# Layer 0's causal mask from a matmul with a constant, and low weight halves on GpSimd

## The chip, the cores and the metric

The kernel runs on one core of a Trainium2 chip. The metric is the device time of one execution in microseconds. A core has five engines with queues of their own that run in order: TensorE (PE, with its weight loads shown apart as PEld), VectorE (DVE), ScalarE (ACT), GpSimd (POOL) and SyncE (SP, which here only issues DMAs).

## The reference

Two layers of a decoder trunk over 512 tokens of width 1024. The change touches the mixer of layer 0 alone: stick-breaking attention of 8 heads of width 64 beside a short convolution of 512 channels, both fed by one projection.

```python
def stick_breaking_attention(q, k, v):
    ...
        z = jnp.einsum('bqhd,bkhd->bhqk', qb, k).astype(jnp.float32) * scale
        mask = kpos[None, :] < qpos[:, None]
        log_beta = jax.nn.log_sigmoid(z)
        log_1m_beta = jnp.where(mask, log_beta - z, 0.0)
        after = lax.cumsum(log_1m_beta, axis=3, reverse=True) - log_1m_beta
        w = jnp.where(mask, jnp.exp(log_beta + after), 0.0)
        return jnp.einsum('bhqk,bkhd->bqhd', w.astype(v.dtype), v)
```

In words: each weight is the sigmoid of its logit times the product of (1 - sigmoid) of all later keys that the query may see. A key at or after the query's own place counts as 1 in the product and as 0 in the weight. After layer 0's mixer come a SwiGLU, layer 1's sparse attention and a second SwiGLU, which the change leaves alone.

## The kernel before

Products are made in three matmuls of fp32r halves: weights and inputs are split into a rounded high half and a low half (`mm3`, L105 to L107; token-major L232 to L234). A weight tile of 128 x 1024 numbers is loaded to `raw`, ScalarE rounds it to `wh` (L162), and an engine takes `raw - wh` to `wl` (L163): VectorE, unless the caller names another in `lo`. `raw`, `wh` and `wl` have three buffers each, and a tile feeds 24 matmuls of 512 columns.

Layer 0's mixer (`layer0_mix`) runs in this order: the queries, then key and value projections (`k_proj`, `proj_tm`), four key tiles in all, then four convolution chunks of three tiles each (`conv_chunk`). The attention heads are a generator (`stick`) that is stepped between groups of three projection matmuls, so that heads and projection share every engine's queue. For a head and a block of 128 queries, `first` makes the logits `z` on TensorE (L507, L508), two sigmoids on ScalarE (`om` = 1 - sigmoid, L525, and `be` = sigmoid, L526), two masks on GpSimd on the diagonal block (L528: 1 into `om`, 0 into `be`) and a column of ones (L531), then a scan of products over `om` (L532) and the product with `be` (L535) on VectorE. `second` turns `be` on TensorE (`pt`, L552), splits it (`wth` on ScalarE, L184; `wtl` on VectorE, L185) and multiplies by the values (`po`, L562, L563); ScalarE and VectorE then take `po` out (`ptmp`, `o`). `k_proj` scales its product to `kt` (L648) and lays each of two heads' keys into both halves of the partitions: one half by ScalarE (L651), the other by GpSimd (L652); VectorE makes the low half (L653).

A tile framework sets the order of most of this stage by its own estimates; the engines then run their queues in that order. `plan` cuts the first key tile and the first value tile ahead, on VectorE.

Of the kernel before, what the change touches and what calls it, by code (L numbers as in the profile page):

```python
# [8 lines left out]
F32 = mybir.dt.float32  # L9
F32R = mybir.dt.float32r  # L10
ALU = mybir.AluOpType
# [65 lines left out]
class Net:  # L77
# [238 lines left out]
    def setup(self):  # L316
        nc, I = self.nc, self.I
        cst = self.cst
        self.ones = cst.tile([P, P], F32, name="ones")
        nc.vector.memset(self.ones, 1.0)  # L320
        self.zero = cst.tile([P, 1], F32, name="zero")
        nc.vector.memset(self.zero, 0.0)
        self.ssq = cst.tile([P, S], F32, name="ssq")
        one = self.ssq[:, 2 * P:3 * P]
        nc.gpsimd.affine_select(out=one, in_=self.ones, pattern=[[-1, P]],
                                compare_op=ALU.is_equal, fill=0.0, base=0, channel_multiplier=1)
        self.eye = cst.tile([P, P], F32R, name="eye")
        nc.vector.tensor_copy(self.eye, one)
        self.ident = self.eye.bitcast(F32)
        self.xT = cst.tile([P, KC, S], F32, name="xT")  # L330
        self.rbc = cst.tile([P, S], F32, name="rbc")
        self.rcol = cst.tile([P, TB], F32, name="rcol")
        self.rq = cst.tile([P, 2 * TB], F32, name="rq")
        self.arena = cst.tile([P, int(ARENA_KB * 256)], F32R, name="arena")

        rows, self.rows2 = self.ssq[0:16, 0:P], self.ssq[0:32, P:2 * P]
        self.cols = cst.tile([P, 48], F32, name="cols")
        nc.scalar.dma_start(rows, I["norm_mix"].rearrange("l (c p) -> (l c) p", p=P))
        nc.scalar.activation(self.rcol[:, 0:1], self.zero, AF.Copy, scale=self.ones[:, 0:1])

        warm = self.bank("z", "pstat")
        for i in range(WARM):
            nc.tensor.matmul(warm[:, 0:P], self.ones, self.ones, start=True, stop=True)
        ps = self.bank("z", "pstat")
        nc.tensor.transpose(ps[:, 0:16], rows, self.ident[0:16, 0:16])
        nc.vector.tensor_copy(self.cols[:, 0:16], ps[:, 0:16])
# [163 lines left out]
    def stick(self, heads, keys, sp, state):  # L510


        nc = self.nc
        outs = {}

        def first(h, qb, ws):
            i, e = h // 2, h % 2
            qs, (kd, kl) = heads[i], keys[i]
            nk = (qb + 1) * P
            t = slice(qb * P, nk)  # L520
            z = self.bank("z", "z")[:, 0:nk]
            self.qk(z, qs[:, e, t], kd[:, e, 0:nk], kl[:, e, 0:nk])
            om = sp.tile([P, nk + 1], F32, name="om", tag=f"om{qb}", bufs=1)
            be = sp.tile([P, nk], F32, name="be", tag=f"be{qb}", bufs=2)
            nc.scalar.activation(om[:, 0:nk], z, AF.Sigmoid, scale=self.rq[:, qb:qb + 1])  # L525
            nc.scalar.activation(be, z, AF.Sigmoid, scale=self.rq[:, TB + qb:TB + qb + 1])  # L526
            for tile_, fill in ((om, 1.0), (be, 0.0)):
                nc.gpsimd.affine_select(out=tile_[:, t], in_=tile_[:, t], pattern=[[-1, P]],  # L528
                                        compare_op=ALU.is_gt, fill=fill, base=0,
                                        channel_multiplier=1)  # L530
            nc.gpsimd.memset(om[:, nk:nk + 1], 1.0)  # L531
            nc.vector.tensor_tensor_scan(om[:, 0:nk][:, ::-1], om[:, 0:nk][:, ::-1],  # L532
                                         self.zero.to_broadcast([P, nk]), initial=1.0,
                                         op0=ALU.mult, op1=ALU.add)
            nc.vector.tensor_tensor(be, be, om[:, 1:nk + 1], op=ALU.mult)  # L535
            ws[qb] = be

        def second(h, ws):
            i, e = h // 2, h % 2
            rows = slice(64 * e, 64 * e + 64)  # L540
            po = self.bank("c" if h % 2 and state["acc"] else "o", "po")

            def turn(kbs, j):
                self.turns += 1
                pt = self.bank("tb"[self.turns % 2] if state["acc"] else "t", "pt")
                wh = sp.tile([P, S], F32R, name="wth", tag="wth", bufs=4)
                wl = sp.tile([P, S], F32R, name="wtl", tag="wtl", bufs=4)
                n, place = 0, {}
                for kb in kbs:
                    place[kb] = n  # L550
                    for qb in range(kb, TB):
                        nc.tensor.transpose(pt[:, n:n + P], ws[qb][:, kb * P:(kb + 1) * P],  # L552
                                            self.ident)
                        n += P
                self.split((wh[:, 0:n], wh.bitcast(F32)[:, 0:n], wl[:, 0:n]), pt[:, 0:n])
                return wh, wl, place

            def prod(kbs, wh, wl, place):
                for kb in kbs:
                    a = slice(place[kb], place[kb] + (TB - kb) * P)  # L560
                    v = self.vs[:, kb, h]
                    nc.tensor.matmul(po[:, kb * P:], v, wh[:, a], start=kb == 0, stop=False)  # L562
                    nc.tensor.matmul(po[:, kb * P:], v, wl[:, a], start=False, stop=kb == 2)  # L563

            groups = ((0,), (1, 3), (2,))
            t0 = turn(groups[0], 0)
            yield True
            t1 = turn(groups[1], 1)
            yield True
            while not state["v"]:  # L570
                yield False
            prod(groups[0], *t0)
            t2 = turn(groups[2], 0)
            yield True
            prod(groups[1], *t1)
            yield True
            prod(groups[2], *t2)

            if e == 0:
                outs[i] = sp.tile([P, S], F32, name="o", tag="o")  # L580
            tmp = sp.tile([P, S], F32, name="ptmp", tag="ptmp")
            nc.scalar.copy(tmp[rows], po[64:128])
            nc.vector.tensor_tensor(outs[i][rows], po[0:64], tmp[rows], op=ALU.add)
            if e == 1:
                (ah, ahf), al = self.R(32 + 4 * i, S), self.R(34 + 4 * i, S)[0]
                self.split((ah, ahf, al), outs[i])
            yield True

        prev = iter(())
        for h in range(9):  # L590
            ws = {}
            if h < 8:
                while not state["k"] > h // 2:
                    yield False
                for qb in range(TB):
                    first(h, qb, ws)
                    yield True
                    r = next(prev, None)
                    while r is False:
                        yield False  # L600
                        r = next(prev, None)
                    if r:
                        yield True
            yield from prev
            prev = second(h, ws) if h < 8 else None

    def layer0_mix(self):
# [28 lines left out]
        with self.tc.tile_pool(name="l0", bufs=1) as sp:  # L636
# [5 lines left out]
            def k_proj(i):  # L642
                b = 64 + 8 * (i % 3)
                (kd, kdf), kl = self.R(b, 2, S), self.R(b + 4, 2, S)[0]

                def ev_k(m, ps):
                    kt = sp.tile([P, S], F32, name="kt", tag="ct0")
                    nc.vector.tensor_tensor(kt, ps, self.rbc, op=ALU.mult)  # L648
                    for e in range(2):
                        own, oth = slice(64 * e, 64 * e + 64), slice(64 - 64 * e, 128 - 64 * e)  # L650
                        nc.scalar.copy(kd[own, e], kt[own])  # L651
                        nc.gpsimd.tensor_copy(kd[oth, e], kt[own])  # L652
                        nc.vector.tensor_tensor(kl[own, e], kt[own], kdf[own, e], op=ALU.subtract)  # L653
                self.proj_fm(W, 512 + i * P, P, xs, ev_k, gcols=P, per=8)
                return kd, kl

            conv = []
# [3 lines left out]
            def conv_chunk(j):  # L661
# [24 lines left out]
                    self.split((ah, ahf, al), y)  # L686

                for col, ev in ((2048, ev_c), (2560, ev_u), (1536, ev_b)):
                    self.proj_fm(W, col + j * P, P, xs, ev, gcols=P, per=8)
                conv.append((ah, al))  # L690

            def more_keys():
# [3 lines left out]
            for i in range(4):  # L696
# [4 lines left out]
                    self.few_banks(None)  # L701
                self.after(LAG0, more_keys)
                if i == 0:
                    self.proj_tm(W, 1024, xs, ev_v)
                    self.after(LAG0, lambda: state.update(v=True))
                    self.few_banks("ad")
                    state["acc"] = True
# [532 lines left out]
```

## Time and profile before

| what | us |
|---|---|
| median of three runs (1211.82 to 1212.19) | 1211.86 |
| the profiled execution | 1214.13 |
| its span on the core | 1212.4 |
| TensorE busy in the span | 1189.0 |
| VectorE, ScalarE, GpSimd busy | 652.9, 480.1, 143.8 |

A row of a group of instructions gives line, engine, operation, tiles written and read, shape, count, then busy time and mean nanoseconds of one, then the idle time of that engine just before them and what ended it. A row of the timeline gives start, duration, engine, line, operation and tiles. Durations of matmuls overlap: what one costs in a stream is the distance to the next start.

### The profile page before, as it was taken

The page shows a single profiled execution, that of the slowest core. Times are in us where ns is not written, and L with a number is a line of the kernel's source. Part 1 is how long each engine was busy: PE and PEld are TensorE (multiplying, and loading weights), DVE is VectorE, ACT ScalarE, POOL GpSimd, SP SyncE. Part 2 cuts the span into 40 slices and gives each one's busy share as a digit, 9 for nine tenths or more (in the row PEclk, how much of TensorE's full clock was granted, in tenths as well). Part 3 has the DMA queues.
Part 4 walks back from the last instruction along what each step waited for, and adds up shares of the span by engine and source line. Part 5 has one row for each costly group of instructions (what it writes and reads, how often), then busy time and mean ns, then how long its engine had stood idle before and what let it go on. Part 6 is the DMA issues. An engine that isn't in the chain of part 4 may idle for free.

```text
span 1212.4 us, 14654 instructions
## 1 busy us (share of the span) xinstructions
PE 1189.0 (98%) x5547; PEld 978.5 (81%) x5547; DVE 652.9 (54%) x1067; ACT 480.1 (40%) x797; POOL 143.8 (12%) x217
## 2 busy tenths in 40 slices
PE   9999999999999999999999989999999999999998
PEld 7777878888888888888788868888888888888886
DVE  5679965655545443333379977745444343342222
ACT  5556634543434332222253577534332322322120
POOL 1234300200000000011001554312000000000000
PEclk9999999999999999999999999999999999999999
DMA  5322125878887632232346432223333333332430
GB/s 191 92 70 70 53 84 190 277 248 281 284 273 262 226 92 96 96 96 78 124 150 232 157 104 70 71 78 126 91 89 90 103 87 102 89 104 88 129 97 35
DMA packets 118583, 159.86 MB, mean 132 GB/s; under 512 B 6292, under 2 KB 91840, under 8 KB 118512
## 3 DMA queue, kind: packets, MB, share of 16 engines
q1 hardware_dynamic: 117712, 157.73, 40.1%
q10 hardware_dynamic: 800, 1.18, 0.3%
q8 instruction: 44, 0.72, 0.2%
q14 instruction: 27, 0.22, 0.1%
HBM read 131.00 MB, written 27.89 MB: 131 GB/s over the span
## 4 chain that ended last, share of the span: by engine, by line
PE 89%; DVE 6%; issue 2%; POOL 2%; ACT 0%; DMA 0%; POOLq 0%; DVEq 0%; ACTq 0%
PE acc L105 22%; PE acc L107 21%; PE acc L106 21%; PE acc L234 6%; PE acc L233 6%; PE acc L232 6%; PE pt L1118 1%; PE z L507 1%; PE z L508 1%; DVE om L532 1%; DVE wl L163 1%; PE po L106 1%; PE po L107 1%; DVE be L535 1%; PE po L105 1%
## 5 line engine op out<-in xcount | busy, mean ns | idle before, releaser
L105 PE MATMUL acc<-arena,wh 128*128 128x512 f32 (+2 forms) x1176 | 466.7, 397 | 1.9 <-DVE xT L728 1.0
L107 PE MATMUL acc<-arena,wl 128*128 128x512 f32 (+2 forms) x1176 | 458.2, 390 | 0.1
L106 PE MATMUL acc<-arena,wh 128*128 128x512 f32 (+2 forms) x1176 | 458.0, 389 | 0.0
L163 DVE TENSOR_TENSOR wl<-raw,wh 128x1024 fp32r<-128x1024 f32 (+1 forms) x167 | 202.9, 1215 | 285.3 <-ACT wh L162 285.0
L162 ACT CAST wh<-raw 128x1024 fp32r<-128x1024 f32 (+1 forms) x167 | 173.0, 1036 | 360.5 <-PE acc L106 155.7
L107 PEld LDWEIGHTS acc<-arena,wl 128*128 128x128 f32 (+1 forms) x1176 | 220.4, 187 | 49.9 <-DVE wl L163 0.4
L105 PEld LDWEIGHTS acc<-arena,wh 128*128 128x128 f32 (+1 forms) x1176 | 220.8, 188 | 46.9 <-DVE xT L728 2.1
L106 PEld LDWEIGHTS acc<-arena,wh 128*128 128x128 f32 (+1 forms) x1176 | 220.8, 188 | 43.6 <-issue 0.7
L232 PE MATMUL acc<-wh,arena 128*128 128x512 f32 x272 | 108.8, 400 | 0.0
L234 PE MATMUL acc<-wh,arena 128*128 128x512 f32 x272 | 108.4, 399 | 0.0
L233 PE MATMUL acc<-wl,arena 128*128 128x512 f32 x272 | 108.2, 398 | 0.0
L286 POOL TENSOR_TENSOR ssq<-ssq,sqx 128x512 f32<-128x512 f32 x12 | 18.2, 1520 | 371.7 <-ACT sqx L285 371.7
L234 PEld LDWEIGHTS acc<-wh,arena 128*128 128x128 f32 x272 | 51.5, 189 | 12.2
L815 DVE TENSOR_TENSOR pwl<-praw,pwh 128x1024 fp32r<-128x1024 f32 (+1 forms) x25 | 30.2, 1208 | 57.0 <-ACT pwh L814 57.0
L233 PEld LDWEIGHTS acc<-wl,arena 128*128 128x128 f32 x272 | 51.5, 189 | 11.6
L232 PEld LDWEIGHTS acc<-wh,arena 128*128 128x128 f32 x272 | 51.5, 189 | 11.5
L763 DVE TENSOR_TENSOR ft<-acc,rbc 128x512 f32<-128x512 f32 x44 | 30.0, 690 | 45.7 <-PE acc L107 45.6
L814 ACT CAST pwh<-praw 128x1024 fp32r<-128x1024 f32 (+1 forms) x25 | 25.9, 1036 | 68.5 <-DMA praw<-in_od_w_in_dram 38.2
L765 ACT ACTIVATE fs<-ft 128x512 f32<-128x512 f32 x44 | 27.6, 629 | 51.3 <-DVE ft L763 51.3
L507 PE MATMUL z<-arena 128*128 128x384 f32 (+3 forms) x120 | 40.7, 342 | 6.7 <-DVE mx L1085 4.1
L1085 DVE CUSTOM_DVE_ANT_0 L<-z,bias 128x128 f32<-128x128 f32 (+3 forms) x64 | 30.7, 485 | 22.2 <-PE z L1084 19.6
L770 DVE TENSOR_TENSOR fp<-acc,fs 128x512 f32<-128x512 f32 x44 | 30.4, 690 | 22.7 <-PE acc L107 22.7
(212 smaller groups left out, 1281.0 us busy)
## 6 DMA issues: line engine op xcount, KB each, us to landing
raw<-in_ffn_w_gate_dram SPq DMA_DIRECT2D x44, 512.0 KB, 3.7
raw<-in_ffn_w_up_dram SPq DMA_DIRECT2D x44, 512.0 KB, 3.8
raw<-in_ffn_w_down_dram SPq DMA_DIRECT2D x42, 512.0 KB, 3.7
l1h<-pwh SPq DMA_DIRECT2D x24, 512.0 KB, 2.7
l1l<-pwl SPq DMA_DIRECT2D x24, 512.0 KB, 3.1
wh<-l1h SPq DMA_DIRECT2D x24, 512.0 KB, 4.0
wl<-l1l SPq DMA_DIRECT2D x24, 512.0 KB, 4.5
raw<-in_ev_w_in_dram SPq DMA_DIRECT2D x23, 512.0 KB, 3.9
```

Source lines behind the costliest of these rows:

```text
L105: mm(ps, wh, xh, start=first, stop=False)
L106: mm(ps, wh, xl, start=False, stop=False)
L107: mm(ps, wl, xh, start=False, stop=last)
L162: nc.scalar.copy(wh, raw)
L163: (lo or nc.vector).tensor_tensor(wl, raw, wh.bitcast(F32), op=ALU.subtract)
L232: mm(ps[tb], h[:, t], wh[:, k], start=c == 0, stop=False)
L233: mm(ps[tb], h[:, t], wl[:, k], start=False, stop=False)
L234: mm(ps[tb], l[:, t], wh[:, k], start=False, stop=c == kc - 1)
L507: self.nc.tensor.matmul(z, qs, kd, start=True, stop=False)
L770: nc.vector.tensor_tensor(p, ps, sil[m], op=ALU.mult)
L815: nc.vector.tensor_tensor(l, raw, h.bitcast(F32), op=ALU.subtract)
L1085: nc.vector.tensor_tensor_reduce(out=u["ls"][:, r], in0=z, in1=bias[h][:, 0:nk][:, ::-1], scale=1.0, scalar=FILL, op0=ALU.add, op1=ALU.max ...
```

## The change

The diagonal mask becomes a third matmul into the logits: the identity (`eye`) times a constant `ahead` that holds -1e30 at and above the diagonal. The sigmoids then give 1 and 0 there by themselves. The GpSimd masks and the 32 small memsets go; four `om` tiles get their ones once. The low halves of key tiles 1 to 3, value tiles 1 to 3 and all twelve convolution tiles go from VectorE to GpSimd: 18 tiles (the two that are cut ahead stay). For the first key tile the copy to the other half of the partitions goes from GpSimd to VectorE.

```diff
+        far = self.ssq[:, 3 * P:4 * P]
+        nc.gpsimd.memset(far, 0.0)
+        nc.gpsimd.affine_select(out=far, in_=far, pattern=[[-1, P]], compare_op=ALU.is_gt,
+                                fill=NEG, base=0, channel_multiplier=1)
+        self.ahead = cst.tile([P, P], F32R, name="ahead")
+        nc.gpsimd.tensor_copy(self.ahead, far)
...
+        oms = [sp.tile([P, (qb + 1) * P + 1], F32, name=f"om{qb}", bufs=1) for qb in range(TB)]
+        for qb in range(TB):
+            nc.gpsimd.memset(oms[qb][:, (qb + 1) * P:], 1.0)
...
-            self.qk(z, qs[:, e, t], kd[:, e, 0:nk], kl[:, e, 0:nk])
-            om = sp.tile([P, nk + 1], F32, name="om", tag=f"om{qb}", bufs=1)
+            self.qk(z, qs[:, e, t], kd[:, e, 0:nk], kl[:, e, 0:nk], False)
+            nc.tensor.matmul(z[:, t], self.eye, self.ahead, start=False, stop=True)
+            om = oms[qb]
...
-            for tile_, fill in ((om, 1.0), (be, 0.0)):
-                nc.gpsimd.affine_select(out=tile_[:, t], in_=tile_[:, t], pattern=[[-1, P]],
-                                        compare_op=ALU.is_gt, fill=fill, base=0,
-                                        channel_multiplier=1)
-            nc.gpsimd.memset(om[:, nk:nk + 1], 1.0)
...
-                        nc.gpsimd.tensor_copy(kd[oth, e], kt[own])
+                        (nc.gpsimd if i else nc.vector).tensor_copy(kd[oth, e], kt[own])
...
-                self.proj_fm(W, 512 + i * P, P, xs, ev_k, gcols=P, per=8)
+                self.proj_fm(W, 512 + i * P, P, xs, ev_k, gcols=P, per=8, lo=nc.gpsimd)
...
-                    self.proj_fm(W, col + j * P, P, xs, ev, gcols=P, per=8)
+                    self.proj_fm(W, col + j * P, P, xs, ev, gcols=P, per=8, lo=nc.gpsimd)
...
-                    self.proj_tm(W, 1024, xs, ev_v)
+                    self.proj_tm(W, 1024, xs, ev_v, lo=nc.gpsimd)
```

Line numbers of the changed kernel are 6 or 7 higher. TensorE's queue at the first head's logits, before (`acc` is the value projection, 128x128 and 128x256 the first two query blocks):

```order
L507 MATMUL z<-arena 128x128
L507 MATMUL z<-arena 128x256
L234 MATMUL acc<-wh,arena 128x512
L232 MATMUL acc<-wh,arena 128x512
L233 MATMUL acc<-wl,arena 128x512
L234 MATMUL acc<-wh,arena 128x512
L508 MATMUL z<-arena 128x128
L508 MATMUL z<-arena 128x256
```

The same place after:

```order
L513 MATMUL z<-arena 128x128
L513 MATMUL z<-arena 128x256
L234 MATMUL acc<-wh,arena 128x512
L232 MATMUL acc<-wh,arena 128x512
L514 MATMUL z<-arena 128x128
L534 MATMUL z<-ahead,eye 128x128
L514 MATMUL z<-arena 128x256
L534 MATMUL z<-ahead,eye 128x128
```

Two projection matmuls that stood ahead of the second logit product now stand behind it, and each block has its mask matmul. By the fourth turned block (`pt`) 20 projection matmuls have gone since the first logit before, 13 after. From the second head's last logits on, heads and projection stand in the same order in both, to within one matmul, but for the mask matmuls.

VectorE's queue in the first convolution chunk, before:

```order
L675 TENSOR_TENSOR cg<-acc,ct 128x512
L163 TENSOR_TENSOR wl<-raw,wh 128x1024
L678 SCALAR_TENSOR_TENSOR cy<-cg,cols,cy 128x512
L532 SCALAR_TENSOR_TENSOR om<-om,zero 128x384
L680 SCALAR_TENSOR_TENSOR cy<-cg,cols,cy 128x512
L535 TENSOR_TENSOR be<-be,om 128x384
L682 TENSOR_TENSOR cy<-cy,rbc 128x512
L185 TENSOR_TENSOR wtl<-pt,wth 128x256
```

And after:

```order
L682 TENSOR_TENSOR cg<-acc,ct 128x512
L539 SCALAR_TENSOR_TENSOR om_408<-om_408,zero 128x384
L685 SCALAR_TENSOR_TENSOR cy<-cg,cols,cy 128x512
L542 TENSOR_TENSOR be<-be,om_408 128x384
L687 SCALAR_TENSOR_TENSOR cy<-cg,cols,cy 128x512
L185 TENSOR_TENSOR wtl<-pt,wth 128x256
L689 TENSOR_TENSOR cy<-cy,rbc 128x512
```

The weight's low half is gone from the queue, and the scan and the low half of the turned block stand one place earlier among the convolution's own steps. GpSimd's queue from the first `om` memset on, before:

```order
L531 MEMSET om 128x1 x4
L672 MEMSET cg 128x2
L652 CAST arena<-kt 64x512 x2
L528 AFFINE_SELECT om<-om 128x128
L528 AFFINE_SELECT be<-be 128x128
L528 AFFINE_SELECT om<-om 128x128
L531 MEMSET om 128x1
```

And after, where `wl` are the weights' low halves:

```order
L163 TENSOR_TENSOR wl<-raw,wh 128x1024 x2
L524 MEMSET om_406 128x1
L524 MEMSET om_407 128x1
L524 MEMSET om_408 128x1
L524 MEMSET om_409 128x1
L679 MEMSET cg 128x2
L163 TENSOR_TENSOR wl<-raw,wh 128x1024 x4
L659 CAST arena<-kt 64x512 x2
L163 TENSOR_TENSOR wl<-raw,wh 128x1024
```

Two low halves of value tiles stand ahead of the memsets; the third value tile's stands right behind them.

## The prediction

> **What bounds the kernel now.** I read the page's busy totals first, then a table of stretches around the changed stage, then TensorE's waits there.
>
> ```profile
> span 1212.4 us, 14654 instructions
> PE 1189.0 (98%) x5547; PEld 978.5 (81%) x5547; DVE 652.9 (54%) x1067; ACT 480.1 (40%) x797; POOL 143.8 (12%) x217
> 43.50:62.00 18.50, 15.58 (x66) 11.29 (x66) 10.81 (x18) 8.59 (x15) 7.60 (x20) 0.91 0.23 65
> 62.00:108.00 46.00, 44.07 (x213) 35.70 (x214) 39.11 (x56) 28.81 (x51) 18.81 (x41) 1.00 0.24 69
> 108.00:161.00 53.00, 50.84 (x264) 41.77 (x263) 50.69 (x79) 33.72 (x64) 17.05 (x47) 1.00 0.21 60
> 161.00:275.00 114.00, 114.00 (x499) 93.14 (x498) 67.75 (x78) 49.42 (x61) 9.59 (x7) 1.00 0.65 214
> ...
> PE po L563 <- DVE wtl L185: 2.9, 3, 1.4
> PE pt L552 <- DVE be L535: 2.1, 4, 0.6
> ```
>
> In a row of stretches come start and end, length, busy time of PE, PEld, DVE, ACT, POOL, then TensorE's granted clock. TensorE is the bound everywhere, so a change gains only by closing its idle time and loses by each matmul that it adds. The heads of layer 0 run from 43.5 to 161 us. There TensorE is idle 18.5 - 15.58 = 2.9 us in the first stretch (at a clock of 0.91) and 46 - 44.07 + 53 - 50.84 = 4.1 us in the two others; behind 161 us it has no gap. So about 7 us plus the slow clock is all that can be had. The two wait rows (from 43.5 to 165 us; total, times, longest) say who ends most of the gaps: VectorE's two results for the turned blocks, 5.0 us. One GpSimd copy, below, ends the rest. VectorE is the close second: 39.11 + 50.69 = 89.8 us busy of 99.
>
> **The mask matmuls.** 32 are added, one for each head and block. Their price is the distance between starts in a stream. The same form stands in layer 1, a constant times the identity:
>
> ```profile
> 700.80 0.30 PE L507 MATMUL z<-arena 128*128 128x128 f32 x1 [0.35 <-DVE mx L1085]
> 700.93 0.28 PE L508 MATMUL z<-arena 128*128 128x128 f32 x1
> 701.04 0.28 PE L507 MATMUL z<-arena 128*128 128x128 f32 x1
> 702.77 0.28 PE L508 MATMUL z<-arena 128*128 128x256 f32 x1
> 702.89 0.28 PE L1084 MATMUL z<-mask,eye 128*128 128x256 f32 x1
> ```
>
> Starts 0.11 to 0.13 us apart for 128 columns, 0.12 for 256: the narrow ones are no cheaper than the wide. I take 0.11, so 32 x 0.11 = 3.5 us; the low end is half of the 256-column distance, 32 x 0.06 = 1.9, the high end 32 x 0.13 = 4.2. All 32 lie in TensorE's stream, so they are paid unless they fall into a gap.
>
> **What leaves GpSimd and VectorE.**
>
> ```profile
> L163 DVE TENSOR_TENSOR wl<-raw,wh 128x1024 fp32r<-128x1024 f32 x15 | 19.5, 1301 | 2.6 <-ACT wh L162 2.6
> L528 POOL TENSOR_SCALAR_AFFINE_SELECT be<-be 128x128 f32<-128x128 f32 x32 | 19.2, 598 | 5.0 <-ACT be L526 4.5
> L528 POOL TENSOR_SCALAR_AFFINE_SELECT om<-om 128x128 f32<-128x128 f32 x32 | 13.5, 422 | 23.3 <-ACT om L525 23.1
> L532 DVE TENSOR_TENSOR_SCAN om<-om,zero 128x128 f32<-128x128 f32 (+3 forms) x32 | 26.8, 839 | 4.7 <-POOL om L528 2.7 <-POOL om L531 1.9
> L535 DVE TENSOR_TENSOR be<-be,om 128x128 f32<-128x128 f32 (+3 forms) x32 | 15.6, 490 | 2.2 <-POOL be L528 0.4
> ```
>
> These are groups from 43.5 to 165 us. Off GpSimd go 19.2 + 13.5 us of masks; VectorE's scans and products stop waiting for it (4.7 and 0.4 us). Off VectorE go 18 low halves at 1.22 us free of contention (a row below) to 1.30, some 22 us, of which I count 12 between 62 and 161 us: 14.7 us. By that alone VectorE would fall from 89.8 to 75 us of 99.
>
> **What the low halves cost on GpSimd.** No such operation of 128 x 1024 stands in the trace. The nearest are
>
> ```profile
> L1030 POOL TENSOR_TENSOR arena<-qt,arena 128x512 fp32r<-128x512 f32 x4 | 5.2, 1292 | 6.4 <-ACT arena L1029 6.4
> 213.07 1.64 POOL L286 TENSOR_TENSOR ssq<-ssq,rbc 128x512 f32<-128x512 f32 x1 [1.73 <-ACT rbc L285]
> 213.47 1.79 DVE L188 SCALAR_TENSOR_TENSOR arena<-xT,cols,arena 128x512 fp32r<-128x512 f32 x1
> L188 DVE SCALAR_TENSOR_TENSOR arena<-acc,rcol,arena 128x512 fp32r<-128x512 f32 x4 | 3.0, 749 | 1.9 <-ACT arena L187 1.9
> L188 DVE SCALAR_TENSOR_TENSOR arena<-xT,cols,arena 128x512 fp32r<-128x512 f32 x8 | 7.0, 875 | 1.6 <-ACT arena L187 1.6
> 81.02 2.16 POOL L652 CAST arena<-kt 64x512 fp32r<-64x512 f32 x2 [3.07 <-DVE kt L648]
> 81.04 1.66 DVE L163 TENSOR_TENSOR wl<-raw,wh 128x1024 fp32r<-128x1024 f32 x1 [0.16 <-ACT wh L162]
> 49.89 1.22 DVE L163 TENSOR_TENSOR wl<-raw,wh 128x1024 fp32r<-128x1024 f32 x1
> L163 DVE TENSOR_TENSOR wl<-raw,wh 128x1024 fp32r<-128x1024 f32 x21 | 26.3, 1253 | 12.0 <-ACT wh L162 11.8
> L653 DVE TENSOR_TENSOR arena<-kt,arena 64x512 fp32r<-64x512 f32 x8 | 7.4, 929 | 0.1
> L498 DVE TENSOR_TENSOR arena<-acc,arena 64x512 fp32r<-64x512 f32 x8 | 5.5, 689 | 0.2
> ```
>
> A subtraction of 128 x 512 takes 1.29 us, so twice the width lies between 2.1 (a part of it fixed) and 2.6; I take 2.4. As work this is hidden: 18 x 2.4 = 43 us on an engine that loses 33, and a tile has 24 matmuls at 0.23 us, 5.5 us, with three buffers ahead. But the two engines do not run beside each other. At 213.47 us a VectorE instruction that takes 0.75 us (the row of four) lasts 1.79: it reads two SBUF tiles, and GpSimd's operation ends at 214.71, whereafter it still needs 0.55. At 81.04 the low half lasts 1.66 in place of 1.22 while GpSimd copies. So a low half on GpSimd holds up VectorE's scans and products for up to 2.4 us, where on VectorE it took 1.22. How often? The bounds are these. In the calmer stage from 161 to 275 us (the row of eight and the row of 21) VectorE lost 8 x (0.875 - 0.749) = 1.0 us and 21 x (1.253 - 1.22) = 0.7 to six GpSimd operations of 1.3 us: a fifth of the hold. To the eight key copies of about half a microsecond it lost 3.2 us (8 x (0.929 - 0.689) in L653 and three times some 0.43 in L163): three quarters. With 12 x 2.4 = 29 us of hold that is 6 to 22 us; I take 60%, 17 us, nearer to the upper row because VectorE is as full here as there. VectorE then stands at 75 + 17 = 92 us against 89.8: its relief is spent. I therefore leave TensorE's 4.1 us of gaps as they are, less 1.2 us because some 25 mask matmuls (2.8 us) now give a late VectorE that much more time. Ends: -3.6 with VectorE at 81 us, +5 with it at 97.
>
> The Trainium skill says this in "SBUF — State Buffer" (section on the engines' ports): GpSimd and a VectorE instruction with two SBUF inputs take one shared pair of ports under an exclusive lock, for the whole instruction. The trace agrees, with the 1.79 us above. Taken by that rule for every hold, VectorE's queue would lose 29 us, and the sum would be that of the second rival below.
>
> **The first head.** Its gap is the copy of the first key tile.
>
> ```profile
> 49.28 0.69 DVE L648 TENSOR_TENSOR kt<-acc,rbc 128x512 f32<-128x512 f32 x1 [2.90 <-DMA F<-ft]
> 49.53 0.21 POOL L531 MEMSET om<- 128x1 f32 x4 [45.13 <-DMA F<-ft]
> 50.11 2.49 POOL L652 CAST arena<-kt 64x512 fp32r<-64x512 f32 x2 [0.33 <-DVE kt L648]
> 51.62 0.50 PE L507 MATMUL z<-arena 128*128 128x128 f32 x2 [1.76 <-POOL arena L652]
> 62.07 0.33 PE L552 MATMUL pt<-eye,be 128*128 128x128 f32 x1 [0.62 <-DVE be L535]
> ```
>
> With the copy on VectorE behind `kt` (ends 49.97), the first logits could start near 50.6, 1 us sooner, and the mask hop is gone from the chain to the fourth turned block (62.07). But GpSimd's third value half now stands behind the `om` memsets and starts near 49.8, as `kt` ends, and holds the ports until 52.2; the copy and the logits then come near 52.5. Two low halves of the keys follow on VectorE (0.69 each), so the first logits are whole near 54; one sigmoid on, four scans and four products take 26.8 / 8 + 15.6 / 8 = 5.3 us and their hand-offs some 0.5, so the fourth turned block comes near 60.3, with 7 fewer projection matmuls done (1.6 us): as good as 61.9 now. I take -0.2; the ends are -2.2 (the copy isn't held up) and +1.
>
> **The sum:** +3.5 (mask) - 1.2 (gaps filled) - 0.2 (first head) = +2.1 us on the profiled execution (1214.13 us, span 1212.4, so 1.7 around it). That execution is 2.3 us above the median of 1211.86, and the difference is carried over: 1214.0. The rest of the kernel, 275 us on, is untouched. The added set-up on GpSimd (a memset, a mask, a copy, near 1 us) lies beside TensorE's warm-up; were that cover gone it would cost that microsecond.
>
> **Rivals.** *VectorE is relieved after all.* For it: the 14.7 us less in its queue, the scans' 4.7 us of waiting gone, and the row of eight, a fifth of the hold. Then the gaps of 62 to 161 us close to about 0.5 (-3.6) and the first head gains up to 2.2: 3.5 - 3.6 - 2.2 = -2.3, and with the mask at 1.9, -3.9: 1208 to 1210. Against it stands the VectorE row of 1.79.
>
> *The holds bind VectorE.* Once its queue is full, the next instruction is mostly a scan or product, and each hold costs the whole 2.4: 75 + 29 = 104 us of work in a stretch of 99. It decides from about 85% held. With the idle time that waiting on ScalarE leaves, the stretch grows by 5 to 9 us: 1217 to 1221. Against it: VectorE's steps that read PSUM (`wtl`, `kt`, `o`) run through a hold.
>
> *GpSimd itself is late*, with the low halves, or with key copies queued behind one. For it, the copy's 2.49 us for two. Against it, a tile each 121.5 / 15 = 8 us and a margin of two tiles. A microsecond at each of three key tiles: 1217.
>
> **Chances.** My forecast (waits about as now, masks paid; +0.5 to +4.5) 45%; relief 32%; holds that bind 18%; late GpSimd 5%. What a measurement can tell from no change here is about 0.2%, 2.4 us. Of the forecast's cases 26 lie within it and 19 above; of the relief's 22 below it and 10 within; the other two are slower but for a share of 1 that falls below. So faster 0.23, same 0.36, slower 0.41 after rounding. The range is 1208.5 to 1219.5: the relief's lower price and most of the binding case are in it. The forecast alone has 1212.4 to 1216.4.
>
> **What would show it.** Right: TensorE's busy time from 43.5 to 161 us up by about 3.5, 18 low halves on GpSimd of 2.4 us or longer, VectorE's scans and products lengthened to 2 us and more where they meet one, waits of TensorE on `wtl` and `be` still near 5 us, the first logits later than 51.6. Wrong: scans at their present lengths and no TensorE waits (relief), or TensorE gaps of more than 8 us in the heads (binding). The mask's price is wrong if `z` matmuls of 128 columns start less than 0.08 us apart.

## The result, and the profile after

The changed kernel takes 1225.31 us (median; 1224.70 to 1225.95), the kernel before on the same chip 1212.03 (1211.82 to 1214.35): a ratio of 1.0105, 95% interval 1.0088 to 1.0123. The forecast was 1214.0 with a range to 1219.5, so the time lies outside it. The profiled execution of after has a span of 1224.2 us, 11.8 longer than that of before.

The first lines of the page of after:

```profile
span 1224.2 us, 14580 instructions
...
PE 1195.2 (98%) x5579; PEld 983.1 (80%) x5579; DVE 658.0 (54%) x1051; ACT 479.8 (39%) x797; POOL 150.6 (12%) x144
```

GpSimd works 6.8 us more, VectorE 5.1 us *more* although 18 low halves of 1.2 us have left it. The stretches of after (start and end, length, busy time of PE, PEld, DVE, ACT, POOL, TensorE's clock); the heads now last until 174 us:

```profile
43.50:62.00 18.50, 14.81 (x64) 10.54 (x64) 10.52 (x16) 8.03 (x15) 4.91 (x7) 0.91 0.21 61
62.00:108.00 46.00, 44.07 (x219) 35.94 (x218) 35.19 (x44) 27.05 (x48) 19.82 (x12) 1.00 0.21 60
108.00:174.00 66.00, 59.02 (x304) 47.46 (x303) 60.85 (x80) 36.39 (x67) 17.86 (x10) 1.00 0.22 63
174.00:287.00 113.00, 113.00 (x495) 92.43 (x494) 67.52 (x73) 49.12 (x60) 14.34 (x9) 1.00 0.64 215
```

The last stretch in before, made as long, for comparison:

```profile
108.00:174.00 66.00, 63.84 (x322) 52.36 (x321) 59.36 (x90) 38.32 (x70) 17.15 (x48) 1.00 0.22 64
```

TensorE is idle 3.7 + 1.9 + 7.0 = 12.6 us in the heads; it was 7.0 before. Its clock is 0.91 in the first stretch, as before. From 174 to 287 us it has no gap, as before. VectorE is no busier than it was: 35.2 + 60.9 = 96.0 of 112 us against 39.1 + 59.4 = 98.5. TensorE's waits from 43.5 to 175 us (total, times, longest):

```profile
PE po L570 <- DVE wtl L185: 4.6, 8, 2.0
PE pt L559 <- DVE be L542: 3.7, 5, 1.4
PE z L513 <- DVE arena L659: 2.1, 1, 2.1
PE pt L559 <- DVE wtl L185: 1.2, 1, 1.2
PE pstat L365 <- DMA ssq<-in_od_k_gain_dram: 0.8, 1, 0.8
```

The two results of VectorE that the forecast named end 9.5 us of waiting in place of 5.0. The groups of GpSimd and VectorE in the same stretch:

```profile
L163 POOL TENSOR_TENSOR wl<-raw,wh 128x1024 fp32r<-128x1024 f32 x15 | 37.4, 2491 | 69.9 <-ACT wh L162 67.3 <-PE acc L106 2.4
L539 DVE TENSOR_TENSOR_SCAN om<-om,zero 128x128 f32<-128x128 f32 (+3 forms) x32 | 34.9, 1090 | 3.1 <-ACT om L537 3.0
L542 DVE TENSOR_TENSOR be<-be,om 128x128 f32<-128x128 f32 (+3 forms) x32 | 21.5, 672 | 2.6
```

A low half takes 2.49 us on GpSimd on average. The scans go from 839 to 1090 ns, the products from 490 to 672, with their waits for GpSimd's masks gone. The longest wait shows how one hold travels (timeline of after: start, duration, engine, line):

```profile
168.02 2.36 POOL L163 TENSOR_TENSOR wl<-raw,wh 128x1024 fp32r<-128x1024 f32 x1 [6.16 <-ACT wh L162]
167.65 0.67 DVE L677 TENSOR_TENSOR ct<-acc,rbc 128x512 f32<-128x512 f32 x1
168.35 2.58 DVE L678 TENSOR_TENSOR ct<-ct,rbc 128x512 f32<-128x512 f32 x1
170.86 1.27 DVE L185 TENSOR_TENSOR wtl<-pt,wth 128x512 fp32r<-128x512 f32 x2
169.19 0.40 PE L569 MATMUL po<-wth,arena 128*128 128x512 f32 x1
171.59 0.50 PE L570 MATMUL po<-wtl,arena 128*128 128x512 f32 x1 [2.01 <-DVE wtl L185]
```

GpSimd's low half runs from 168.02 to 170.38. VectorE's `ct`, with both inputs in SBUF, begins inside it and ends at 170.9; in before it takes 0.67 to 0.69 us. Behind it in the queue stands `wtl`, which reads PSUM and would not itself be held: four `wtl` of after begin inside a low half, and each takes within 0.04 us of its shortest time. TensorE, which had three projection matmuls between the turn and the second value product, stands still for 2.0 us.

### The profile page after: what moved, and what is told of

It reads as the page before. It is cut to its first block, busy times and chain, and to the rows that moved or that the text cites. A ratio compares the mean times of both kernels' runs of the same rounds, so it can differ in the third digit from the quotient of the medians.

```text
span 1224.2 us, 14580 instructions
## 1 busy us (share of the span) xinstructions
PE 1195.2 (98%) x5579; PEld 983.1 (80%) x5579; DVE 658.0 (54%) x1051; ACT 479.8 (39%) x797; POOL 150.6 (12%) x144
## 4 chain that ended last, share of the span: by engine, by line
PE 86%; DVE 9%; issue 1%; POOL 1%; ACT 1%; DMA 0%; ACTq 0%; DVEq 0%; POOLq 0%
PE acc L105 21%; PE acc L107 21%; PE acc L106 21%; PE acc L234 6%; PE acc L233 6%; PE acc L232 6%; DVE om L539 2%; DVE be L542 1%; PE pt L1125 1%; PE z L513 1%; PE z L514 1%; DVE wtl L185 1%; PE po L106 1%; DVE arena L504 1%; DVE arena L660 1%
## 5 line engine op out<-in xcount | busy, mean ns | idle before, releaser
L163 DVE TENSOR_TENSOR wl<-raw,wh 128x1024 fp32r<-128x1024 f32 (+1 forms) x149 | 179.9, 1208 | 286.1 <-ACT wh L162 285.9
L163 POOL TENSOR_TENSOR wl<-raw,wh 128x1024 fp32r<-128x1024 f32 x18 | 44.6, 2476 | 112.1 <-ACT wh L162 109.5
L777 DVE TENSOR_TENSOR fp<-acc,fs 128x512 f32<-128x512 f32 x44 | 30.4, 691 | 24.8 <-PE acc L107 24.8
```

What stands on the lines that cost most here:

```text
L163: (lo or nc.vector).tensor_tensor(wl, raw, wh.bitcast(F32), op=ALU.subtract)
L777: nc.vector.tensor_tensor(p, ps, sil[m], op=ALU.mult)
```

## The experiments

Two theories. *Holds*: an instruction of GpSimd that reads SBUF holds VectorE's next step with two SBUF inputs, and the length of that one hold goes straight into the chain scan, product, turn, `wtl`, TensorE. Rivals: the mask matmuls, or the moved copy, make the loss; or VectorE is short of time in all, so that the sum of the holds counts.

**The two parts apart.** Mask matmuls alone, all low halves on VectorE; the first key copy stays on VectorE (against after; the key and convolution calls likewise):

```diff
-                    self.proj_tm(W, 1024, xs, ev_v, lo=nc.gpsimd)
+                    self.proj_tm(W, 1024, xs, ev_v)
```

> The mask by matmul and the first key copy on VectorE stay; all 18 low halves go back to VectorE. Theory (held ports: a low half on GpSimd keeps VectorE's scans and products waiting for 2.4 us at a time): the loss of 13 us goes with them. What is left is at most 3.5 us of mask matmuls less the mask's waits: 1211 to 1215 us. Rival (the matmuls in TensorE's stream and the new order at the first head cost it): it stays at 1221 to 1225 us.

Low halves alone, masks left on GpSimd (against before; the other calls likewise):

```diff
-                    self.proj_tm(W, 1024, xs, ev_v)
+                    self.proj_tm(W, 1024, xs, ev_v, lo=nc.gpsimd)
```

> The kernel before with nothing but the 18 low halves on GpSimd: its masks, memsets and key copies stay there too. Held ports: at least the 13 us of the changed kernel, and more, since the masks now also stand in GpSimd's queue behind low halves of 2.4 us: 1225 to 1245 us. Rival (mask matmuls and order cost it, low halves on GpSimd are hidden): 1209 to 1214 us.

The masks alone: 1212.22 us, a ratio of 0.9991 (0.9982 to 1.0001). The low halves alone: 1230.18 us, 1.0137 (1.0117 to 1.0158). So the low halves make the whole loss, and with the masks still on GpSimd more than the whole. Stretches of the kernel with the masks alone:

```profile
43.50:62.00 18.50, 16.92 (x82) 12.19 (x81) 13.45 (x24) 10.52 (x20) 0.25 (x5) 1.00 0.37 103
62.00:108.00 46.00, 44.20 (x221) 36.14 (x219) 37.27 (x52) 27.07 (x47) 6.43 (x6) 1.00 0.20 58
108.00:161.00 53.00, 53.00 (x285) 44.54 (x284) 50.05 (x79) 33.72 (x63) 0.20 (x2) 1.00 0.22 63
```

TensorE is idle 3.4 us where before it was 7.0. So 3.6 us of idle time are gone, about what the mask matmuls cost (3.5), and the first stretch runs at full clock. Which part of the edit wins the idle time was not tried apart: VectorE's scans no longer wait for GpSimd's masks (4.7 us before), and TensorE's wait for the first key copy falls from 1.8 to 0.8 us.

**The copy of the first key tile** back on GpSimd (against after):

```diff
-                        (nc.gpsimd if i else nc.vector).tensor_copy(kd[oth, e], kt[own])
+                        nc.gpsimd.tensor_copy(kd[oth, e], kt[own])
```

> The changed kernel with the first key tile's copy back on GpSimd. In the changed kernel that copy was held 2.0 us on VectorE by GpSimd's third value half. Held ports: on GpSimd it stands behind the same low half and comes no sooner: within 1.5 us of the changed kernel's 1225.3. Rival (the copy's move to VectorE is what is late): the first head's 2.7 us come back, 1222 to 1223 us.

1224.37 us, 1.0102 (1.0079 to 1.0126): no measurable difference from after, so the rival of the moved copy is out. On either engine the copy stands beside or behind the same value half.

**Convolution tiles only** on GpSimd, keys and values on VectorE (against after; the key call likewise):

```diff
-                    self.proj_tm(W, 1024, xs, ev_v, lo=nc.gpsimd)
+                    self.proj_tm(W, 1024, xs, ev_v)
```

> The changed kernel with the low halves of keys and values back on VectorE; only the 12 of the convolution on GpSimd. Held ports: the holds up to the second head go (0.75 us at the set-up copy, 2.7 us to the first product with the values, and a part of the third and fourth head's), those of the later heads stay: 1218 to 1221 us. Rival (the early ones make all of the loss by delaying the chain of heads as a whole): 1212 to 1214 us.

1221.73 us, 1.0073 (1.0052 to 1.0094), a little above what was expected. About 9.5 us for twelve holds (against the masks alone), so the loss is spread over the heads and not made at one place.

**Is it reading, or any work of GpSimd?** The low halves stay on VectorE, and GpSimd works twice on each of the 18 spent `raw` tiles: by filling it, which only writes, or by copying it onto itself, which reads (against the masks alone; in the second `tensor_copy(raw, raw)` stands for the memset).

```diff
+        if lo is not None:
+            for _ in range(2):
+                nc.gpsimd.memset(raw, 0.0)
```

> All low halves on VectorE (as in the first experiment, 1212.2 us), and behind each of the 18 two GpSimd memsets of the spent raw tile, work that the result doesn't need, about 1 us each, which read nothing from SBUF. If it is the reading that holds VectorE's steps with two SBUF inputs: 1211 to 1215 us and scans at their free lengths. The rival (any GpSimd work beside the scans holds them, or takes their place in the order): as much as with copies, 1217 us or more. The Trainium skill (SBUF — State Buffer, the section on SBUF's two separate sides) has it that such a VectorE step is locked only against a GpSimd operation that reads SBUF; by it the lower figure holds.

> As the kernel with two memsets, but with two GpSimd copies of the raw tile onto itself, about 1 us each, which read and write SBUF. Held ports: 36 holds of 1 us with VectorE still doing the low halves: scans and products of up to 1 us more than free, 1216 to 1226 us. Rival (GpSimd's length of work in the way of the low halves, not ports): as with memsets, 1211 to 1215 us.

Groups of the filling kernel, GpSimd's in the whole span and VectorE's scans in the heads:

```profile
L166 POOL MEMSET raw<- 128x1024 f32 x36 | 34.5, 957 | 108.4 <-DVE wl L163 50.7 <-DMA ssq<-in_od_k_gain_dram 35.3 <-ACT wth L187 14.6
L542 DVE TENSOR_TENSOR_SCAN om<-om,zero 128x128 f32<-128x128 f32 (+3 forms) x32 | 25.9, 815 | 0.6 <-ACT om L540 0.5
```

The same of the copying kernel, with TensorE's two largest waits in the heads:

```profile
L166 POOL COPY raw<-raw 128x1024 f32<-128x1024 f32 x36 | 47.8, 1328 | 108.4 <-DVE wl L163 40.8 <-DMA ssq<-in_od_k_gain_dram 36.5 <-ACT wth L187 22.6
L542 DVE TENSOR_TENSOR_SCAN om<-om,zero 128x128 f32<-128x128 f32 (+3 forms) x32 | 30.4, 955 | 0.1
...
PE po L573 <- DVE wtl L188: 5.5, 4, 2.6
PE pt L562 <- DVE be L545: 3.3, 3, 2.2
```

Filling: 1211.95 us, 0.9997 (0.9987 to 1.0007), scans at 815 ns as without it. Copying: 1222.72 us, 1.0084 (1.0069 to 1.0099), scans at 955 ns. So it is GpSimd's reading of SBUF that holds VectorE. The Trainium skill states this in "SBUF — State Buffer" (section "Who interferes with whom"): a VectorE instruction with two SBUF inputs contends with a GpSimd instruction that reads SBUF, not with one that only writes it. These two runs agree. It isn't the fills' shorter time (0.96 us against 1.33): subtractions of 0.85 us, the quarters below, lengthen VectorE's steps, and the fills don't.

**One hold's length, or their sum?** The low half is cut along its columns into 2, 4, 8 or 16 instructions; the number is the only difference (against after). TensorE, VectorE and ScalarE keep the same instructions in the same order in all of them.

```diff
+        for j in range(8):
+            c = slice(j * kk * n // 8, (j + 1) * kk * n // 8)
+            lo.tensor_tensor(l2[:, c], r2[:, c], h2[:, c], op=ALU.subtract)
```

> The changed kernel with each low half on GpSimd in two instructions of 128x512, some 1.29 us each, with the same order in the other queues. If the length of one hold decides: between whole tiles (1225.3) and quarters (1217.6), 1219 to 1223, with TensorE's waits on wtl and be near 5 us in the heads. If the sum of hold time decides (2.58 in place of 2.40 us a tile): 1225 to 1227.

> The changed kernel with each low half on GpSimd cut into four instructions of 128x256, about 0.7 us each (a little more work in all). Held ports, for the length of one instruction: VectorE's longest scans and products fall from some 2.5 us to below 2, and since it also gets its own instructions in between, TensorE's waits shrink: 1217 to 1223 us. Rival (the ports are shared by volume, or GpSimd's lateness is what counts): the same time or a little worse, 1225 to 1228 us.

> The low halves on GpSimd cut into eight instructions of 128x128, 0.4 us each, so 3.2 us of holds for a tile in place of 2.4. If the length of one hold is what delays TensorE (a scan or product late by a whole instruction): again faster than with quarters (1217.6), 1213 to 1216 us. If it is the sum of time for which the ports are held: slower than with quarters, 1219 to 1225 us.

> The changed kernel with each low half on GpSimd cut into sixteen instructions of 128x64; TensorE's, VectorE's and ScalarE's queues keep their order. One piece takes about 0.3 us by the 0.46 us of 128x128 and the 1.29 us of 128x512 (an estimate), so a tile needs some 5 us in place of 2.4. If the length of one hold decides: no slower than eighths, 1208.5 to 1211.5. If the sum of GpSimd's hold time decides: it is now the largest of all, over 90 us, and the time is that of the changed kernel or more, 1225 to 1232. If GpSimd's own lateness sets in (a tile every 8 us, pieces lengthened to 0.5 us by VectorE): 1213 to 1217, with TensorE waiting on wl.

| instructions for a tile | median ns of one | their time on GpSimd, us | VectorE steps lengthened by, us | TensorE idle 43.5 to 174, us | time, us | ratio to before (95%) |
|---|---|---|---|---|---|---|
| 1 (after) | 2406 | 44.6 | 24.8 | 12.6 | 1225.31 | 1.0105 (1.0088 to 1.0123) |
| 2 | 1300 | 53.3 | 21.7 | 7.6 | 1220.14 | 1.0064 (1.0051 to 1.0078) |
| 4 | 848 | 69.0 | 16.4 | 5.5 | 1217.62 | 1.0033 (1.0018 to 1.0049) |
| 8 | 471 | 94.7 | 8.6 | 1.6 | 1210.26 | 0.9980 (0.9971 to 0.9989) |
| 16 | 322 | 126.0 | 9.0 | 1.7 | 1210.44 | 0.9981 (0.9972 to 0.9990) |

"Lengthened by" sums, over VectorE's steps from 30 to 175 us, what each took above the shortest of its shape in any of these kernels, where that is over 0.06 us; in before it is 5.6 us. GpSimd's time doubles from the first row to the fourth, and the loss goes away. So it isn't the sum of GpSimd's time that counts, but how long one instruction is: the rival by sums expected 1225 us and more for halves and for sixteenths. Quarters lie within the holds theory's range, eighths 3 us below it: it had not seen that the total lengthening would fall too.

These rows alone therefore don't part one long hold from VectorE's lost time as a whole. Against the latter stand the stretches of after, where VectorE is busy for less than before and TensorE idles for longer. Nor is the length of a hold all: in the copying kernel no step is lengthened by more than 0.87 us, and all by 17.4, less than with halves (1.15 and 21.7), yet TensorE idles 10.1 us from 43.5 to 174 against 7.6. VectorE still makes the low halves there, 127.8 us of work from 30 to 175 us against 117.2. A fuller queue leaves less room for the same hold; that was not tried by itself.

Stretches, then GpSimd's group and TensorE's waits in the heads, of the kernel with eighths:

```profile
43.50:62.00 18.50, 17.20 (x88) 13.08 (x87) 13.99 (x23) 11.41 (x21) 12.33 (x27) 1.00 0.26 73
62.00:108.00 46.00, 46.00 (x235) 38.35 (x234) 33.13 (x51) 27.97 (x50) 35.01 (x56) 1.00 0.24 69
108.00:161.00 53.00, 52.66 (x277) 43.85 (x276) 44.79 (x67) 32.52 (x61) 34.48 (x51) 1.00 0.24 70
```

```profile
L169 POOL TENSOR_TENSOR wl<-raw,wh 128x128 fp32r<-128x128 f32 x144 | 89.7, 657 | 66.6 <-ACT wh L162 66.3
...
PE pt L565 <- DVE be L548: 1.4, 3, 0.7
PE z L519 <- ACT be L544: 0.2, 1, 0.2
```

TensorE's waits on `wtl` are gone and those on `be` are down to 1.4 us. With 16 pieces nothing more is won. Eighths and sixteenths beat the kernel before by 0.2%. The interval of the masks alone (0.9982 to 1.0001, on another chip) overlaps with theirs, so that the low halves in eighths add a gain to that of the masks is likely and not shown.

**Two variants of eighths.** The value tiles back on VectorE (against eighths):

```diff
-                    self.proj_tm(W, 1024, xs, ev_v, lo=nc.gpsimd)
+                    self.proj_tm(W, 1024, xs, ev_v)
```

> Low halves of keys and convolution in eighths on GpSimd, those of the value tiles back on VectorE. If the holds of set-up and first head (the 32x128 copy there, the first key copy) still cost in eighths: 0.5 to 1 us below eighths of all, 1209.0 to 1210.0. If the three value halves, 1.22 us each, are dearer in VectorE's queue ahead of the first head: 1210.5 to 1212.

Before's masks on GpSimd with the low halves in eighths there too (against the kernel with the low halves alone):

```diff
-        (lo or nc.vector).tensor_tensor(wl, raw, wh.bitcast(F32), op=ALU.subtract)
+        if lo is None:
+            nc.vector.tensor_tensor(wl, raw, wh.bitcast(F32), op=ALU.subtract)
+            return wh, wl
...
+        for j in range(8):
+            c = slice(j * kk * n // 8, (j + 1) * kk * n // 8)
+            lo.tensor_tensor(l2[:, c], r2[:, c], h2[:, c], op=ALU.subtract)
```

> The kernel before with the 18 low halves on GpSimd in eighths, the masks still on GpSimd. GpSimd's work in the heads is then some 82 us of low halves and 33 us of masks in a stretch of 117. If short holds alone bring the gain and the masks cost nothing where they are: 1209.5 to 1211.5. If the mask matmuls are what makes room: masks queue behind up to eight pieces, 1214 to 1222, with VectorE waiting on om and be from GpSimd.

The first: 1211.98 us, 0.9999 (0.9990 to 1.0008), the dearer of its two cases. One value half of 1.22 us stands between `kt` and the key copy there, the first logits start at 51.1 us in place of 50.1, and TensorE idles 3.4 us in the heads for 1.6. The second: 1230.33 us, 1.0149 (1.0136 to 1.0163), above its range. Its timeline on GpSimd and its scans' group:

```profile
84.42 4.38 POOL L169 TENSOR_TENSOR wl<-raw,wh 128x128 fp32r<-128x128 f32 x8
88.76 0.29 POOL L534 TENSOR_SCALAR_AFFINE_SELECT om<-om 128x128 f32<-128x128 f32 x1
89.00 0.29 POOL L534 TENSOR_SCALAR_AFFINE_SELECT be<-be 128x128 f32<-128x128 f32 x1
...
L538 DVE TENSOR_TENSOR_SCAN om<-om,zero 128x128 f32<-128x128 f32 (+3 forms) x32 | 27.8, 870 | 32.1 <-POOL om L534 27.7 <-POOL om L537 4.2
```

The scans are short (870 ns) and yet VectorE stands 27.7 us ahead of them waiting for masks: a mask queues behind all eight pieces of a tile. TensorE idles 17.1 us from 43.5 to 174 us in place of 7.0, and its clock is granted at 0.50 for 13.6 us there in place of 3.4, some 5 us more (an estimate); together that is 15 of the 17.8 us lost. So low halves on GpSimd, even in short pieces, cost nothing only where the masks are off it. The masks' own move doesn't need the low halves (1212.22 us alone).

## Why the prediction was wrong, point by point

**The mask matmuls, +3.5 us: right.** Timeline of after, around the last matmul of one head's logits:

```profile
107.61 0.39 PE L513 MATMUL z<-arena 128*128 128x512 f32 x1
107.84 0.39 PE L514 MATMUL z<-arena 128*128 128x512 f32 x1
108.06 0.22 PE L534 MATMUL z<-ahead,eye 128*128 128x128 f32 x1
108.12 0.45 PE L105 MATMUL acc<-arena,wh 128*128 128x512 f32 x1
108.41 0.40 PE L106 MATMUL acc<-arena,wh 128*128 128x512 f32 x1
```

From 107.84 to 108.41 are 0.57 us for two wide matmuls and a mask, where two take 0.46: 0.11 us for the mask, at this place. The sign I gave for a wrong price, starts less than 0.08 us apart, was ill chosen: the mask's own distance is 0.06, and the next matmul's is longer by as much. That TensorE's busy time of 43.5 to 161 us would rise by 3.5 was no sign either, since its waits lengthened in the same stretch.

**A low half on GpSimd, 2.4 us, and 60% of the hold lost: right.** 2.41 us is the median of the 18. From 62 to 161 us, the stretch of the forecast, VectorE's steps were lengthened by 20.1 us, against 3.2 with the masks alone: 17 us, as forecast, for 30.3 us of low halves, 56%. The way to it was partly luck. The upper of its two bounds, three quarters, took the eight key copies at half a microsecond; the shortest takes 0.61, and together they take 8.9, of which the 3.2 us lost are a third.

**"I therefore leave TensorE's 4.1 us of gaps as they are, less 1.2 us": the step that failed.** I set the held time against the relief in one account of VectorE's time, and the account came out about right (a forecast of 92 against 89.8; measured 96.0 against 98.5 in the longer stretch of 62 to 174 us). But TensorE's gaps behind 62 us went from 4.1 to 8.9 us, where 2.9 were forecast. TensorE does not wait for VectorE's total; it waits for one scan, one product, one `wtl` at a time, and a hold that falls into that chain delays it by up to its whole length, with a few matmuls as the only margin. The relief, 1.2 us here and there in the queue, could win no more than the gaps there were (3.4 us with the masks alone), and a hold makes new ones. The runs with 2 to 16 pieces show it: the shorter one instruction, the less TensorE waits, down to 8 pieces, whatever GpSimd's time in all.

**The first head, -0.2: wrong, and for the reason that I saw.** The value half and the copy stood in the forecast's order, the copy behind it:

```profile
50.72 2.35 POOL L163 TENSOR_TENSOR wl<-raw,wh 128x1024 fp32r<-128x1024 f32 x1
51.06 2.74 DVE L659 CAST arena<-kt 64x512 fp32r<-64x512 f32 x2
53.50 0.47 PE L513 MATMUL z<-arena 128*128 128x128 f32 x2 [2.10 <-DVE arena L659]
61.29 0.33 PE L559 MATMUL pt<-eye,be 128*128 128x128 f32 x1 [0.67 <-DVE be L542]
63.24 0.33 PE L559 MATMUL pt<-eye,be 128*128 128x128 f32 x1 [0.47 <-DVE be L542]
66.52 0.66 PE L559 MATMUL pt<-eye,be 128*128 128x128 f32 x4 [1.20 <-DVE wtl L185]
```

The logits start at 53.50 (52.5 forecast, 51.62 before). I did not count the next half, the second key tile's at 63.29, inside the same head. The first value product of 512 columns starts 4.2 us later than before, of which 1.5 were there ahead of the heads.

**The set-up, hidden: wrong for the values, right for the constant.** I looked at the new constant and not at the value half that falls on the set-up of layer 1's small inputs:

```profile
38.00 2.41 POOL L163 TENSOR_TENSOR wl<-raw,wh 128x1024 fp32r<-128x1024 f32 x1 [32.84 <-ACT wh L162]
39.46 1.02 DVE L358 COPY ssq<-rcol 32x128 f32<-32x128 f32 x1
```

A copy that took 0.21 us in before takes 1.02, a small load behind it comes later, and TensorE waits 0.8 us (`pstat` in the waits above). A further 0.75 us is TensorE's warm-up, 30 matmuls in 6.09 us against 5.34. The added set-up does not make that: the kernel with the copy back on GpSimd has the same set-up and takes 5.24, and the kernel with before's masks and eighths, without it, takes 6.15. With that set-up it is anything from 5.01 to 6.14 us in the kernels here; what sets it isn't shown.

**The rivals.** The binding one had the sign, the place and the cause, but priced it through a full queue, "75 + 29 = 104 us of work in a stretch of 99" and a point of decision at 85% held; VectorE was at 86% of its stretch and 56% held, and the loss was larger than its 1217 to 1221. Late GpSimd did not show: no wait of TensorE in the heads of after is ended by it. The relief came about near its price, 1208 to 1210, once the holds were cut short: 1210.3 with eighths.

The sum after the fact, in the forecast's terms and in the spans of before and after (1212.4 and 1224.2): +3.5 for the masks, +4.8 for the gaps behind 62 us (forecast -1.2), +0.8 of idle time from 43.5 to 62 us (forecast -0.2), +0.75 of warm-up. That is 9.9 of 11.8 us; the rest was not traced. Against the masks alone (1210.2): TensorE's idle time in the heads 12.6 - 3.4 = 9.2, 0.3 by a later start of the heads that is not idle time already counted, and 0.09 x 18.5 = 1.7 by the clock of the first stretch, 11.2 of 14.0 us.

## What to carry to other kernels

When work moves to GpSimd, list which of its instructions read SBUF and how long each one is, and set that length against the slack of the chain that VectorE feeds, not against VectorE's total idle time. If the work must go there, cut it into pieces shorter than that slack (here 0.5 us did, 0.85 did not), and keep what others wait for out of the same queue. A lighter engine is no relief if what is waited for comes in later lumps.

## What the runs showed of the hardware

Cutting a held operation shortened the holds in all, not only each one: 24.8 us of lengthening with 18 instructions, 8.6 with 144, though GpSimd was at work twice as long. The pieces wait for VectorE as well: 0.45 us is the shortest of the eighths, 0.66 the mean, 1.46 the longest.

A copy on VectorE, with one SBUF input, is held too (0.21 to 1.02 us, above; in after the first of the first key tile's two copies takes 2.29 us where 0.42 is its shortest), so two SBUF inputs are not the only case. The same section of the Trainium skill says so of copies in a mode that uses both ports. The 1.02 us agrees; in which mode the copy ran, the trace doesn't show.

TensorE's clock was at half for 3.4 us, from 1 us behind a gap of 1.8 us on, in before. Stretches of before:

```profile
49.70:51.60 1.90, 0.16 (x1) 0.00 (x0) 1.90 (x3) 1.55 (x3) 1.54 (x4) 1.00 0.02 4
...
52.60:56.00 3.40, 3.40 (x10) 2.71 (x10) 1.96 (x5) 1.36 (x4) 1.51 (x5) 0.50 0.45 130
```

After had the same behind 2.1 us. The kernel with the low halves alone waited 2.9 us at the same place (`z` on the copy, L652), and its clock was 1.00 in that stretch. So the length of the gap alone does not decide it; "TensorE: Matmul & The Clock Gate" (the Trainium skill, section "HAM oscillation — how this bites in real kernels") names gaps over some 3.4 us; the gap in before was shorter, so the measurement differs, and what decides stays open.
